# One queue in strict turn instead of two queues side by side, in a one-pass gradient of a 268 MB array

## The chip, the cores and the metric

The kernel runs on one core of a Trainium2 chip; the other cores are idle. The metric is device time in microseconds (us).

Some words for what follows. HBM is the large memory that holds input and output, SBUF the core's own memory. Data go between them by 16 DMA engines, which all take part in each transfer. A *packet* is what the profile records as one move of one engine, here mostly 64 KB. A transfer has *landed* when the last of the 16 engines is done with it; the *spread* is the time from the first engine to the last. The *turn* is the place where a queue goes from a load to the store behind it.

## The reference

```python
x = np.random.randn(8192, 8192).astype(np.float32)     # 268 MB
def reference(x):
    return np.gradient(x, axis=1)   # inside: (x[j+1] - x[j-1]) / 2; at both ends: a one-sided difference
```

Each input byte has to be loaded once and each output byte stored once: 536.9 MB in all.

## The kernel before

256 rows are one *set* of 8.39 MB: two rows per partition, 64 KB in each of 128 partitions. There are 32 sets and three slots in SBUF. GpSimd (POOL) puts the four edge differences of each pair of rows aside, VectorE (DVE) makes the halved central difference of the whole set in one pass and in place, and a small copy puts the edges back. Then the set is stored from the same slot.

```python
R, NB, SH = 2, 3, 64            # rows per partition, slots, shift of the input within a slot
# ... slots, semaphores ld[k], st[k] (one per slot), counters ...

def load(i):
    k = i % NB
    if i < NB:
        parts = [(ld[k], 0, R)]
    else:
        nc.sync.wait_ge(ld[(i - 1) % NB], 16 * ld_n[(i - 1) % NB])   # the load before has landed
        nc.sync.wait_ge(st[k], 16 * st_n[k])                         # store i-3 has landed
        parts = [(ld[k], 0, R)] if i < nsets - 1 else [(ld_rows[r], r, 1) for r in range(R)]
    for sem, r0, nr in parts:
        nc.sync.dma_start(out=slots[k][...], in_=x_sets[i, ...]).then_inc(sem, 16)
    ld_n[k] += 1

# work(i, ..., placer, storer, sem): DVE pass, edge copy on `placer`, store issued by `storer`

for i in range(NB):
    load(i)
for i in range(nsets):
    k = i % NB
    if i < nsets - 1:
        ready = put_aside(i, 0, R, ld[k], 16 * ld_n[k])
        placer = nc.scalar if i % 2 else nc.vector
        storer = nc.scalar if i + NB < nsets else nc.sync
        work(i, 0, R, ready, placer, storer, st[k])
        st_n[k] += 1
    else:                                  # the last set goes in two half loads and two half stores
        for r in range(R):
            ready = put_aside(i, r, 1, ld_rows[r], 16)
            work(i, r, 1, ready, nc.vector, nc.sync, st_rows[r])
    if i + NB < nsets:
        load(i + NB)
```

Loads are issued by SyncE (SP), and the stores of sets 0 to 28 by ScalarE (ACT), each on its own queue. The stores of the last three sets are on SP, behind the last load. I write L5 and S5 for the load and the store of set 5.

## Time and profile before

| | before |
|---|---|
| time, median of 3 runs | 1252.09 us (1250.42 to 1253.31) |
| traffic | 536.9 MB, 429 GB/s over the span |
| VectorE busy | 44% of the span |

The head of the page of the kernel before: span, VectorE's busy share, the DMA engines' busy tenths in 40 slices, what they moved in each slice, the packets and the queues (q1 is SP's, q10 is ACT's).

```profile
span 1252.1 us, 254 instructions
...
DVE 554.2 (44%) x51; ACT 4.2 (0%) x16; POOL 15.1 (1%) x37
...
DMA  9999999999999999999999999999999999999998
GB/s 402 435 435 433 433 433 435 435 431 427 435 421 433 431 435 431 435 435 429 433 435 435 435 435 429 431 429 427 429 421 435 431 431 435 433 433 435 376 437 371
DMA packets 9506, 536.88 MB, mean 429 GB/s; under 512 B 1057, under 2 KB 1057, under 8 KB 1057
...
q1 hardware_dynamic: 5328, 293.60, 54.7%
q10 hardware_dynamic: 4176, 243.27, 44.8%
```

The DMA engines are busy in every slice; the last three slices have two low ones (376 and 371 GB/s). The 1056 smallest packets are the semaphore increments: 66 transfers times 16 engines (one more is not the kernel's). The Trainium skill, "DMA: Bandwidth & Descriptors", section "Why a DMA increments its semaphore by 16 and not by 1", says that each of the 16 engines posts its own increment after its own data, and that only the full 16 tells that all has landed. The trace agrees.

Three pieces of the chain of waits of the kernel before (start, length, what): loads land 36 to 42 us apart in the steady part, 38.70 us on average from 209 to 1138 us.

```profile
1062.92 38.63 DMA slot<-in_x_dram
1101.57 36.20 DMA slot<-in_x_dram
1137.78 31.38 DMA slot<-in_x_dram
```

Stretches near the end of the kernel before, the windows view (stretch, length, busy time of three engines with counts, clock, DMA share, GB/s):

```profile
core 0: us, DVE busy (x) ACT busy (x) POOL busy (x), PEclk, DMA share, GB/s
1160.00:1165.00 5.00, 0.00 (x0) 0.00 (x0) 0.00 (x0) 1.00 0.97 419
1165.00:1170.00 5.00, 0.54 (x1) 0.00 (x0) 0.20 (x1) 1.00 0.15 66
1170.00:1175.00 5.00, 5.00 (x1) 0.00 (x0) 0.00 (x0) 1.00 1.09 419
1240.00:1245.00 5.00, 0.00 (x0) 0.00 (x0) 0.00 (x0) 1.00 0.99 426
1245.00:1250.00 5.00, 0.00 (x0) 0.00 (x0) 0.00 (x0) 1.00 0.74 321
```

From 1165 to 1170 us the DMA engines are nearly empty, by this view for 5 x (1 - 66/419) = 4.2 us. S28 and L30 have run out, L31 waits, and S29, though computed, stands behind L31 on SP.

The timeline of the kernel before around this place (start, length, engine, line, operation):

```profile
1169.23 0.20 POOL L84 TENSOR_TENSOR ends<-slot 128x4 f32<-128x4 f32 x1 [31.19 <-DMA slot<-in_x_dram]
...
1170.03 34.81 SPq L118 DMA_DIRECT2D out_dram<-slot  x4
1181.27 5.47 POOL L84 TENSOR_TENSOR ends<-slot 128x2 f32<-128x2 f32 x1 [11.84 <-DMA slot<-in_x_dram]
...
1192.28 3.25 POOL L84 TENSOR_TENSOR ends<-slot 128x2 f32<-128x2 f32 x1 [5.54 <-DMA slot<-in_x_dram]
```

The first line is the landing of L30, the second SP's first store after it has issued L31 at last. The third and fourth are the landings of L31's two halves, 11.0 us apart, where 4.19 MB should take half of a set's 19.3 us.

### The profile page before, as it was taken

Reading aid. Unit: us, or ns where it says so; the run is one execution under the profiler, and the core shown is the slowest. Engines: PE = TensorE matmul, PEld = TensorE weight load, DVE = VectorE, ACT = ScalarE, POOL = GpSimd, SP = SyncE. Lnnn points to the kernel's source line nnn. Section 1 sums busy time; section 2 is a strip of 40 time slices with the busy share of each in tenths; the row PEclk is TensorE's granted clock in tenths of the full one; section 3 lists DMA queues with packets and bytes.
Section 4 is the critical chain, followed back from the end, with each engine's and each line's share of the span. In section 5 each row is a group of like instructions: output and inputs, shape, how many; then the busy total and the mean of one; then the engine's idle time right before and its main releaser. Section 6 shows DMA issues by size and latency. Waiting matters only on the chain.

```text
span 1252.1 us, 254 instructions
## 1 busy us (share of the span) xinstructions
DVE 554.2 (44%) x51; ACT 4.2 (0%) x16; POOL 15.1 (1%) x37
## 2 busy tenths in 40 slices
DVE  2841553345542455333554235543355523555640
ACT  0000000000000000000000000000000000000000
POOL 0000000000000000000000000000000000000110
DMA  9999999999999999999999999999999999999998
GB/s 402 435 435 433 433 433 435 435 431 427 435 421 433 431 435 431 435 435 429 433 435 435 435 435 429 431 429 427 429 421 435 431 431 435 433 433 435 376 437 371
DMA packets 9506, 536.88 MB, mean 429 GB/s; under 512 B 1057, under 2 KB 1057, under 8 KB 1057
## 3 DMA queue, kind: packets, MB, share of 16 engines
q1 hardware_dynamic: 5328, 293.60, 54.7%
q10 hardware_dynamic: 4176, 243.27, 44.8%
q14 instruction: 2, 0.01, 0.0%
HBM read 268.44 MB, written 268.44 MB: 429 GB/s over the span
## 4 chain that ended last, share of the span: by engine, by line
DMA 92%; DVE 4%; issue 0%; POOL 0%; SPq 0%
DMA slot<-in_x_dram 89%; DVE slot L102 4%; DMA out_dram<-slot 3%; DVE slot L116 0%; POOL ends L84 0%; SPq L168 0%; SPq L69 0%; SPq L42 0%
## 5 line engine op out<-in xcount | busy, mean ns | idle before, releaser
L102 DVE CUSTOM_DVE_ANT_0 slot<-slot 128x16382 f32<-128x16382 f32 (+1 forms) x33 | 551.3, 16706 | 649.7 <-POOL ends L84 649.7
L84 POOL TENSOR_TENSOR ends<-slot 128x4 f32<-128x4 f32 (+1 forms) x33 | 14.9, 452 | 1180.2 <-DMA slot<-in_x_dram 1180.2
L116 ACT COPY slot<-ends 128x4 f32<-128x4 f32 x15 | 3.0, 198 | 1110.0 <-DVE slot L102 1110.0
L116 DVE COPY slot<-ends 128x4 f32<-128x4 f32 (+1 forms) x18 | 3.1, 171 | 0.6
L116 ACT ACT_TABLE_LOAD x1 | 1.3, 1283 | 41.3 <-DVE slot L116 41.3
L157 POOL MEMSET const-bfloat16-1.0<- 128x1 bf16 x1 | 0.1, 102 | 0.0
L157 POOL MEMSET const-uint8-127<- 128x1 uint8 x1 | 0.1, 102 | 0.0
L157 POOL MEMSET const-float32-0.0<- 128x1 f32 x1 | 0.1, 99 | 0.2 <-issue 0.2
L157 POOL MEMSET const-float32-1.0<- 128x1 f32 x1 | 0.1, 99 | 0.0
## 6 DMA issues: line engine op xcount, KB each, us to landing
slot<-in_x_dram SPq DMA_DIRECT2D x2, 4096.0 KB, 17.3
out_dram<-slot SPq DMA_DIRECT2D x2, 4096.0 KB, 45.3
slot<-in_x_dram SPq DMA_DIRECT2D x31, 38.6
out_dram<-slot ACTq DMA_DIRECT2D x29, 40.2
out_dram<-slot SPq DMA_DIRECT2D x2, 42.8
```

The lines of the kernel that those rows point to most:

```text
L84: nc.gpsimd.tensor_sub(out=ends[:, i, r0 : r0 + nr, :], in0=xin[:, :, 1 : m : m - 2], in1=xin[:, :, 0 : m - 1 : m - 2],),
L102: nc.vector._custom_dve(dve_ops.TENSOR_TENSOR_REDUCE_SUB_MAX, out=mid, in0=after, in1=before, s0=0.0, s1=0.5,),
L116: at = done(copy(out=to, in_=of), placed[placer])
L157: nc = _bacc.Bacc("TRN2", target_bir_lowering=False, num_devices=1)
```

## The change

Its intent is to have loads and stores take strict turns on one queue, with fewer instructions and without waits that the queue's order makes needless.

```diff
             else:
-
-                nc.sync.wait_ge(ld[(i - 1) % NB], 16 * ld_n[(i - 1) % NB])
                 nc.sync.wait_ge(st[k], 16 * st_n[k])
@@
             if i < nsets - 1:
                 ready = put_aside(i, 0, R, ld[k], 16 * ld_n[k])
-                placer = nc.scalar if i % 2 else nc.vector
-                storer = nc.scalar if i + NB < nsets else nc.sync
-                work(i, 0, R, ready, placer, storer, st[k])
+                work(i, 0, R, ready, nc.scalar, nc.sync, st[k])
                 st_n[k] += 1
@@
-            if i + NB < nsets:
-                load(i + NB)
+
+            if i > 0 and i - 1 + NB < nsets:
+                load(i - 1 + NB)
```

The queue's order is now L0 L1 L2 S0 S1 L3 S2 L4 S3 L5 and so on; at the end S29, L31 in two halves, S30, S31 in two halves.

## The prediction

> **What bounds the kernel now.** The DMA engines. The page's slice table shows DMA at 9 in 39 of 40 slices; the whole is 536.9 MB at 429 GB/s. VectorE is busy 44%. In the chain of waits, load landings follow each other every 38.70 us from 209 to 1138 us (24 sets of 16.78 MB, 433.6 GB/s). The Trainium skill, "DMA: Bandwidth & Descriptors", section "Where 436 GB/s comes from", gives a ceiling of 435.2 GB/s; the trace agrees (two loads alone land 19.32 us apart in the timeline, 434 GB/s). 536.9 MB at 435.2 GB/s is 1233.6 us, so 18.5 us is all there is to win.
>
> **Where those 18.5 us are.** Start: the first load lands at 23.1 us, 3.8 more than its 19.3. End: in the last 82.1 us (from the issue at 1170.0) 33.55 MB move, 77.1 us at the ceiling: 5.0 us of latency and completion. Just before, 1165 to 1170 moves 66 GB/s (windows view), about 4.2 us empty: store 28 and load 30 had run out, and everything else stood behind load 31, which waits for store 28. Some 6 us are spread: short dips (229 GB/s in 62 to 64 us), 0.15 us per set.
>
> **What changes.** All stores move from ACT's queue to SP's; the wait of a load for the load before goes; load i+2, not i+3, is issued after store i. The queue's order is S1 L3 S2 L4 S3 L5... Edge copies of all sets but the last go to ACT (0.198 us, not 0.171), off the path.
> - Does the queue run dry? With 19.3 us per transfer, store 3 is issued some 19 us after load 3 landed (POOL 0.20, DVE 17.22, copy 0.2, hops), with load 4 (and store 2) ahead. Load 5 is issued when store 2 lands, again with load 4 ahead: 17 us or more of work stays queued. At the start loads 1 and 2 cover computation 0; at the end store 30 covers the last 8.68 us. The 4.2 us gap disappears.
> - Do turns lower the rate? Before, the engines should alternate between two busy queues packet by packet (same page, "Queues, rings and completion order"; packets are mostly 64 KB), so each already switched direction many times per set and lost 0.15 us. Loads alone ran at 434 GB/s, and the last 82 us already are one SP queue, two half loads and four stores, at the ceiling. Some 60 changes of direction should cost almost nothing.
>
> **Sum (estimate from trace durations).** 64 transfers of 19.32 us are 1236.5, plus 3.8 start, plus about 1 after the last landing: 1241.3. I predict **1242 us**, range **1237 to 1250**. Faster by over 2% needs 1227 us, less than the traffic at the ceiling: chance 0.01. Within 2%: 0.95. Slower: 0.04.
>
> **What would show each step.** Right: ACT's queue gone; landings of loads 38.6 us apart; no slice at 376 near the end; 433 to 435 GB/s nearly everywhere; SP waits for stores and edge copies while DMA never empties. Wrong on starvation: SP waiting for the edge copy while the DMA share falls. Wrong on turns: 39 us or more between landings with DMA at 9, or a dip at each change of direction.
>
> **What would make it wrong.** A fixed drain at each change of direction: 0.3 us each cancels the gain, 0.7 us makes it over 1% slower. Engines drifting apart, so that the slowest decides each landing (the last half loads land 11.0 us apart, not 9.6). A bounded ring holding up SP. Pure writes to HBM slower than mixed traffic; the tail's 58 us of stores say no.

## More of the kernel before

The time of a run is 1.7 to 2.2 us longer than its span, from its first to its last instruction (for instance 1253.98 us of time for a profiled span of 1252.1 us).

## The result, and the profile after

| | before | after |
|---|---|---|
| time, median of the runs beside each other | 1252.70 us (1250.42 to 1256.05, 4 runs) | 1252.36 us (1251.24 to 1252.88, 4 runs) |
| ratio, 95% interval | | 0.9994 (0.9970 to 1.0018) |
| span of the profiled run | 1252.1 us | 1249.5 us |

A ratio is the mean time of one kernel's fast runs over that of the other's of the same rounds, so it is not quite the ratio of the medians. A later set of five rounds gave 0.9991 (0.9977 to 1.0005). The change is worth nothing that these runs can tell; the intervals leave room for 0.3%.

The head of the page of the changed kernel:

```profile
span 1249.5 us, 225 instructions
...
DMA  9999999999999999999999999999999999999997
GB/s 403 436 436 418 428 430 436 434 430 436 432 436 434 436 434 432 432 432 420 434 436 432 434 436 432 436 434 436 436 430 436 436 434 422 428 436 436 436 434 330
DMA packets 9505, 536.88 MB, mean 430 GB/s; under 512 B 1056, under 2 KB 1056, under 8 KB 1056
...
q1 hardware_dynamic: 9504, 536.88, 99.5%
```

ACT's queue is gone. The slice of 376 GB/s near the end is gone too; 436 and 434 stand where the kernel before had 376 and 437. But the last slice fell from 371 to 330. Some pieces of the chain of waits of the changed kernel; each starts at the landing of a load:

```profile
120.79 0.07 issue
...
159.90 0.07 issue
...
472.33 0.07 issue
...
899.83 0.07 issue
...
938.50 0.07 issue
```

The first two are neighbours, 39.11 us apart; from 120.79 to 472.33 us there are nine sets, 39.06 us each, more than the 38.6 that I had predicted. The last two are neighbours again, 38.67 us apart. Something costs 0.4 us per set in the first third of the run and nothing in the last. The same five stretches as before, in the changed kernel:

```profile
1160.00:1165.00 5.00, 0.00 (x0) 0.00 (x0) 0.00 (x0) 1.00 0.97 419
1165.00:1170.00 5.00, 0.00 (x0) 0.00 (x0) 0.00 (x0) 1.00 1.00 433
1170.00:1175.00 5.00, 4.38 (x1) 0.00 (x0) 0.20 (x1) 1.00 0.97 419
1240.00:1245.00 5.00, 0.00 (x0) 0.00 (x0) 0.00 (x0) 1.00 0.38 164
1245.00:1250.00 5.00, 0.00 (x0) 0.00 (x0) 0.00 (x0) 1.00 0.07 28
```

The empty place at 1165 us is gone, as predicted. But from 1240 to 1250 us the engines move little for almost ten microseconds. That is not a gap, as there is nothing left to issue: some engines have finished and some have not.

The 16 landing times of each transfer, taken from the trace, show it plainly. This is the time between the first and the last of the 16 engines to finish a load in the changed kernel, and the total by which the packets near that load's end are longer than the usual 2.418 us, summed over the engines, for ten of the loads:

```
load landed at us       62.5  120.8  159.9  198.8  277.4  433.2  628.0  822.5 1015.8 1131.6
first to last engine     0.4    0.5    0.9    1.2    2.5    3.5    5.2    6.4    6.5    6.5
excess, sum of engines  16.4    4.6    1.2    1.4    4.5    1.7    0.6    2.6    0.0    0.1
```

The excess packets are not anywhere in the run: apart from small ones in the first 260 us, all groups of packets longer than 2.45 us are the last packets of a load, just where the queue turns from a load to the store behind it. At the first such turn all 16 engines lose about 1 us. Later turns hit the engines unequally. The engines come apart, and once they are 6.5 us apart, nearly no packet is long any more (the largest later sum is 1.1 us, at 938 us).

What that does to the end, from the 16 landings of the very last transfer:

| last transfer | mean of the 16 engines | last engine | last minus mean |
|---|---|---|---|
| before | 1249.9 us | 1250.3 us | 0.4 us |
| after | 1243.3 us | 1247.7 us | 4.4 us |

The average engine did gain 6.6 us: 3.2 of idle time in the gap, 3.3 of stretched packets (6.9 us per engine after the first 20 us before, 3.6 after), and 0.1 of small items. The kernel is over when the last engine is, and that one gained 2.6.

### The profile page after: what moved, and what is told of

Same layout as the page of the kernel before. It is cut to its first block, busy times and chain, and to the rows that moved or that the text cites. A ratio compares the mean times of both kernels' runs of the same rounds, so it can differ in the third digit from the quotient of the medians.

```text
span 1249.5 us, 225 instructions
## 1 busy us (share of the span) xinstructions
DVE 551.7 (44%) x35; ACT 7.4 (1%) x32; POOL 6.8 (1%) x37
## 4 chain that ended last, share of the span: by engine, by line
another core or an unknown queue 78%; DMA 15%; DVE 3%; POOL 0%; issue 0%; ACT 0%; SPq 0%
DMA slot<-in_x_dram 9%; DMA out_dram<-slot 7%; DVE slot L100 3%; POOL ends L82 0%; ACT slot L114 0%; DVE slot L114 0%; SPq L165 0%; SPq L42 0%
## 5 line engine op out<-in xcount | busy, mean ns | idle before, releaser
L114 ACT COPY slot<-ends 128x4 f32<-128x4 f32 x31 | 6.1, 198 | 1179.8 <-DVE slot L100 1179.8
L82 POOL TENSOR_TENSOR ends<-slot 128x4 f32<-128x4 f32 (+1 forms) x33 | 6.6, 199 | 1202.2 <-DMA slot<-in_x_dram 1202.2
```

The source lines that it names most:

```text
L82: nc.gpsimd.tensor_sub(out=ends[:, i, r0 : r0 + nr, :], in0=xin[:, :, 1 : m : m - 2], in1=xin[:, :, 0 : m - 1 : m - 2],),
L114: at = done(copy(out=to, in_=of), placed[placer])
```

## The experiments

The theories, as they stood before the runs. **T (turns):** the last packets of a load are stretched where the queue turns from load to store, as long as the engines are in step; the loss is unequal, so that the engines come apart and the slowest decides the end. **D (drift):** some engines are simply slower, whatever the direction. **W (warm-up):** the stretching belongs to the first 800 us of a run. Fourteen kernels were run; "right" means that the output agreed with the reference.

### All transfers loads

```diff
             storer.wait_ge(*at)
+            if i < nsets - 1:      # wrong output on purpose: a load of the same set instead of its store
+                storer.dma_start(out=b[:, r0 * m : (r0 + nr) * m],
+                                 in_=x_sets[i, :, r0 * m : (r0 + nr) * m]).then_inc(sem, 16)
+                return
             storer.dma_start(out=out_sets[...], in_=b[...]).then_inc(sem, 16)
```

> The changed kernel with the stores of all sets but the last turned into loads of the same 8 MB into the same slot (wrong output on purpose): same queue, same dependencies, same bytes, one change of direction in the whole run. Theory T (in the changed kernel the last load packet of an engine is stretched by up to 1.2 us when the queue turns from a load to a store, the less the further the 16 engines are apart, and this costs the slowest engine 6.5 us): the 16 engines stay within 1 us of each other, nearly no 64 KB packet after the first 20 us is longer than 2.45 us, landings 19.34 us apart, span about 1243 (one turn at the end, up to 1 us). Rival D (some engines are simply slower, whatever the direction): the spread of the 16 landings grows to about 6.5 us again and the span is about 1249.5.

### All transfers stores

```diff
             for sem, r0, nr in parts:
+                if i >= NB:        # wrong output on purpose: a store of the slot instead of a load
+                    nc.sync.dma_start(out=out_sets[i, :, r0 * m : (r0 + nr) * m],
+                                      in_=slots[k][:, SH + r0 * m : SH + (r0 + nr) * m]).then_inc(sem, 16)
+                    continue
                 nc.sync.dma_start(out=slots[k][...], in_=x_sets[i, ...]).then_inc(sem, 16)
```

> The changed kernel with all loads but the first three turned into stores of the same slot (wrong output on purpose): one turn, after the third load. Theory T: one stretch of about 1 us per engine at that turn, then none; spread of the landings below 1.5 us to the end; landings 19.34 us apart; span about 1243. Rival D: spread grows to about 6.5 us, span about 1249.5. Rival S (stores to HBM are slower than loads): landings over 19.5 us apart with all engines together.

Measured, one each: 1246.10 us with loads alone and 1246.14 us with stores alone. Their outputs are wrong, which doesn't matter for the times. From the pages, the one with loads first:

```profile
span 1244.3 us, 225 instructions
...
GB/s 404 438 438 430 413 438 438 438 438 438 438 413 430 438 438 438 438 438 419 423 438 438 438 438 438 426 417 438 438 438 438 438 430 413 438 438 438 438 438 371
...
HBM read 528.48 MB, written 8.39 MB: 431 GB/s over the span
```

```profile
span 1244.4 us, 225 instructions
...
GB/s 404 434 430 419 436 438 438 438 438 436 432 423 428 438 438 438 438 438 434 430 419 436 438 438 438 438 434 421 426 438 438 438 438 423 419 438 438 438 438 371
...
HBM read 25.17 MB, written 511.71 MB: 431 GB/s over the span
```

The 16 engines stay 0.3 to 0.5 us apart from 60 us to the end with loads, and 0.6 to 0.9 us with stores; landings are 19.3 us apart in both. With stores, the one turn at 58 us stretched all 16 last load packets, by 16.5 us in sum, and nothing after it was over 0.05 us long. The end of the all-loads run in the windows view:

```profile
1240.00:1245.00 5.00, 0.00 (x0) 0.00 (x0) 0.00 (x0) 1.00 0.25 107
1245.00:1250.00 5.00, 0.00 (x0) 0.00 (x0) 0.00 (x0) 1.00 0.00 0
```

It falls off within 1240 to 1245, where the changed kernel took until 1247.7 us. D is out: with the same bytes, queue and dependencies the engines don't come apart when the queue doesn't turn. (The repeat of the changed kernel ran on another chip; but the kernel with two queues below ran on the same chip as these two, and there the engines came apart.) Loads alone and stores alone are equally fast, so my fear of slow pure writes is out too.

### Kept in step at every turn

```diff
                 nc.sync.wait_ge(st[k], 16 * st_n[k])
+                nc.sync.wait_ge(st[(i - 2) % NB], 16 * st_n[(i - 2) % NB])
```

> The changed kernel, and each load also waits for the newest store, so that the 16 engines run dry and start together before every load-store pair. Theory T: since the engines are in step at every turn, all 16 last load packets are stretched at every turn, about 0.6 to 1.2 us each, to the end of the run, not only in the first 800 us; with some 2 us of emptiness and a slow first packet per pair, landings of loads are 41.5 to 43 us apart instead of 38.7, span 1330 to 1370. Rival W (the stretches belong to the first 800 us of a run and die out by themselves): no stretched packets after 850 us, landings then about 1 us closer together than at the start.

Measured: 1357.97 us, one look, right. Three landings of loads late in the run, from its timeline:

```profile
1060.83 0.20 POOL L83 TENSOR_TENSOR ends<-slot 128x4 f32<-128x4 f32 x1 [42.33 <-DMA slot<-in_x_dram]
...
1103.99 0.20 POOL L83 TENSOR_TENSOR ends<-slot 128x4 f32<-128x4 f32 x1 [42.96 <-DMA slot<-in_x_dram]
...
1146.36 0.20 POOL L83 TENSOR_TENSOR ends<-slot 128x4 f32<-128x4 f32 x1 [42.17 <-DMA slot<-in_x_dram]
```

They are 43.2 and 42.4 us apart, where the changed kernel has 38.7. The engines are 0.4 to 1.0 us apart throughout, and at every turn, to the end, all 16 last load packets are stretched: 16 to 24 us in sum, 1.0 to 1.5 us per engine. As T expected. But it is not quite the same turn as in the changed kernel, since here the queue has run dry before each load; later turns of the changed kernel cost 0.6 to 4.6 us in sum. So W was not out yet; the last two runs below settle that.

### The new order, with the stores on ACT's queue

```diff
-                work(i, 0, R, ready, nc.scalar, nc.sync, st[k])
+                work(i, 0, R, ready, nc.scalar, nc.scalar if i + NB < nsets else nc.sync, st[k])
```

> The changed kernel with its stores, but for the last three sets', issued on ACT's queue again: the new order and the dropped wait of the loads without the one queue. Loads may now run beside stores and ahead of them. Theory T: stretches are now where either direction begins beside the other and not at the end of loads; total cost on the slowest engine of the same kind; time within 0.4% of before (1247 to 1257). If strict turns on one queue mattered by themselves, this would differ from the changed kernel by more than that.

Measured: 1252.47 us (1248.52 to 1257.26, 4 runs), ratio 0.9978 (0.9956 to 1.0001), right. No difference that can be told from the changed kernel, so within some 0.3% the single queue by itself isn't what matters. The profiled run was its slowest (1257.26 us); there the engines were 12.7 us apart at the end, last minus mean 9.9 us, more than in the changed kernel. Two queues do not cure the lag, and here they made it uneven from run to run.

### The changed kernel again

> The changed kernel as it is, to have it beside the next three on one chip. Expected: within 0.4% of before, spread of the 16 landings at the end 6 to 7 us.

Measured: 1251.89 us (1251.03 to 1252.72, 5 runs), ratio 0.9991 (0.9977 to 1.0005). Engines 7.4 us apart at the end (6.5 in the first profile), last minus mean 4.4 us, the same as in the first profile.

### Half as many turns

```diff
-            if i > 0 and i - 1 + NB < nsets:
-                load(i - 1 + NB)
+            if i % 2:
+                for j in (i - 1 + NB, i + NB):
+                    if j < nsets:
+                        load(j)
```

> The changed kernel with the queue's order L L S S L L S S, so half as many turns from load to store (16 instead of 31). Theory T: stretches only at the end of every second load; if each turn adds to the slowest engine what is left until the engines are 6.5 us apart, half as many turns leave the engines 4 to 6.5 us apart at the end and save 0 to 2.5 us (1249 to 1252.5). If the queue ran dry in this order, the span would be over 1255.

Measured: 1251.33 us (1249.87 to 1252.10, 5 runs), ratio 0.9984 (0.9970 to 0.9999), right. Against the 1251.89 of the changed kernel on the same chip it saved half a microsecond, within the noise. Stretches were only at the ends of every second load, as expected, but the engines still ended 6.9 us apart, slightly more than I had expected. The spread grew more slowly (3.6 us at 588 us, where the repeat of the changed kernel had 5.6) and had longer to grow, as stretching went on to the last turn (3.7 us in sum at 1201 to 1206 us). So 16 turns and 31 cost about the same here.

### Half as long packets

```diff
-                parts = [(ld[k], 0, R)]
+                parts = [(ld[k], r, 1) for r in range(R)]        # likewise for the later loads
@@
-            storer.dma_start(out=out_sets[i, :, r0 * m : (r0 + nr) * m], in_=...).then_inc(sem, 16)
+            for r in range(r0, r0 + nr):
+                storer.dma_start(out=out_sets[i, :, r * m : (r + 1) * m], in_=...).then_inc(sem, 16)
```

> The changed kernel with each 8 MB transfer issued as two transfers of one row each, in the same order L L S S per set: same turns, same bytes, packets of 32 KB (1.21 us) instead of 64 KB (2.42 us). Theory T with the spread that ends the stretching counted in packets (6.5 us is 2.7 packets): spread at the end about 3.3 us, time 3 us less than the changed kernel (about 1249). If the spread is a time, not a number of packets: 6.5 us again and no gain.

Measured: 1253.82 us (1252.77 to 1256.13, 5 runs), ratio 1.0014 (0.9997 to 1.0030), right. The spread at the end was 6.3 us, so it is not counted in packets, and my hope of a gain fell. Packets of 32 KB took 1.213 us, which is 0.3% more per byte than 2.418 us for 64 KB; that alone would be some 4 us over 512 packets of 64 KB per engine (an estimate: 512 x 2 x 1.213 = 1242.1 instead of 1238.0). The loss seen is half of that, 1.9 us between the medians. Late in the run, where little is stretched, a set took 38.73 us here and 38.67 us in the repeat of the changed kernel, which over 32 sets is 1.9 us.

### The kernel before, without its gap

```diff
-                storer = nc.scalar if i + NB < nsets else nc.sync
+                storer = nc.scalar
```

> The kernel before with the stores of the last three sets left on ACT's queue, so that they don't stand behind the last load: the gap of 4.2 us at 1165 us should be gone, and nothing else of the change is in. My prediction counted the gap as 4.2 us of time. Theory T: the average engine stood idle there, but the slowest engine for only about 1.3 us (its last packet ends at 1168.8, the next begins at 1170.1), and closing the gap leaves the engines apart to the end: the time falls by 0 to 2 us, not by 4, and the spread at the end is 3 to 9 us instead of 0.6.

Measured: 1248.90 us (1247.39 to 1251.65, 6 runs), ratio 0.9970 (0.9956 to 0.9985), right. This is a miss of my second thoughts: the gap was worth 0.3%, 1.9 to 5.5 us of 1253.5, more than the 0 to 2 expected, and in line with the 4.2 us of the first prediction. The stretch that held the gap, in its windows view:

```profile
1165.00:1170.00 5.00, 0.00 (x0) 0.00 (x0) 0.00 (x0) 1.00 1.03 446
```

It moved 446 GB/s where the kernel before moved 66. The profile fell on its slowest run (1251.65 us), so its ends say little of the faster ones; in it the last half store had to wait for the last half load, which landed only at 1227.6 us beside S30, and the landings of the last transfer were 0.2 us apart, not the 3 to 9 expected (they had been 6.5 us apart at the half load before).

### A copy inside SBUF instead of the store, and a copy inside HBM

```diff
-            storer.dma_start(out=out_sets[i, :, r0 * m : (r0 + nr) * m], in_=b[:, r0 * m : (r0 + nr) * m])
+            inside = i < nsets - 1                       # wrong output on purpose
+            # either: out=b[:, m : 2 * m],  in_=b[:, 0:m]            (SBUF to SBUF, 4 MB)
+            # or:     out=out_sets[i, ...], in_=x_sets[i, ...]       (HBM to HBM, 8 MB)
```

> The changed kernel with the stores of all sets but the last replaced by a copy of one row of the slot onto the other, inside SBUF (4 MB, wrong output on purpose). At the turn that cost 16 us summed over the engines in the changed kernel, the transfers now go from HBM-to-SBUF to SBUF-to-SBUF: only what is read from changes, nothing is written to HBM. Theory Read (the last load packets are stretched because the packets behind them read from SBUF, not from HBM): all 16 last packets of a load before a copy stretched by about 1 us at the first turn. Theory Write (they are stretched because the packets behind them write to HBM): no stretch at the ends of loads.

> The changed kernel with the stores of all sets but the last replaced by copies from the input to the output inside HBM (8 MB, wrong output on purpose). At the turn the transfers go from HBM-to-SBUF to HBM-to-HBM: only what is written to changes. Theory Read: no stretch at the ends of loads. Theory Write: stretched by about 1 us per engine at the first turn. The copies themselves may be slower than stores; the span is not what is looked at.

Measured: 947.69 us with copies inside SBUF (406.9 MB), 1409.73 us with copies inside HBM. Their outputs are wrong, which doesn't matter for the times. Neither theory came through whole. With SBUF copies, all the last load packets were stretched at the first turn (15.0 us in sum), and at none of the later ones, with the engines 0.5 us apart to the end. With HBM copies the last load packets were not stretched at all; the copies were slow from their first packet to their last (a load and a copy landed 44 us apart, so 24.5 us for a copy of 8.39 MB instead of 19.3). The engines came apart all the same, from 0.5 us at the third load to 8.4 us at the end; so they can part without stretched ends of loads, and stretching is the way seen in the changed kernel, not the only one. At the first turn it is enough that the packets behind the load read from SBUF. For the later turns neither reading from SBUF alone nor writing to HBM alone brings the stretching about. What it is that delays the last packets stays open.

### The dropped wait alone

```diff
-                nc.sync.wait_ge(ld[(i - 1) % NB], 16 * ld_n[(i - 1) % NB])     # in the kernel before
```

> The kernel before without the wait of a load for the load before it: one part of the change alone. My sum gave that part no time of its own: within 0.3% of before (1249 to 1257), the gap before the last load still there.

Measured: 1259.08 us (1256.75 to 1262.39, 4 runs), ratio 1.0041 (1.0023 to 1.0059), right. That is 0.4% slower, a little beyond what I had expected. Its windows view near the end:

```profile
1165.00:1170.00 5.00, 0.00 (x0) 0.00 (x0) 0.00 (x0) 1.00 0.09 39
1170.00:1175.00 5.00, 0.00 (x0) 0.00 (x0) 0.00 (x0) 1.00 0.06 26
1175.00:1180.00 5.00, 0.00 (x0) 0.00 (x0) 0.00 (x0) 1.00 0.84 315
```

The thin stretch before L31 has become more than twice as long, and it is lag again: 39 and 26 GB/s is the work of one or two engines (433.7 / 16 = 27 GB/s each). The first engine finished S28 at 1154.8 us and the last at 1175.1; L31 now waits for S28's last engine, and all that is left stands behind L31. So the wait by itself was no cost that could simply be dropped. The changed kernel can drop it because with its queue and its order nothing that is ready stands behind a load that isn't.

### One store more on ACT

```diff
-                storer = nc.scalar if i + NB < nsets else nc.sync      # in the kernel before
+                storer = nc.scalar if i + NB <= nsets else nc.sync
```

> The kernel before with the store of set 29 left on ACT's queue and the last two sets' stores on SP: closes the gap that the last load makes, without the end of the run with every store on ACT, in which the last half load had to share the engines with store 30. Expected: no dip near 1165 us; the engines no longer set equal by the gap, so 3 to 6 us of lag of the slowest engine behind the mean at the end; time 0 to 5 us less than before (about 1249 beside 1253), so about the same as with all three stores on ACT.

Measured: 1250.97 us (1249.39 to 1256.47, 6 runs), ratio 0.9972 (0.9958 to 0.9985), right. As expected: the gap is closed by moving S29 alone, the gain is the same 0.3%, and in the profiled run (again the slowest) the last engine was 3.7 us behind the mean at the end, where the kernel before has 0.4.

### In step once, late, and once, early

```diff
                 nc.sync.wait_ge(st[k], 16 * st_n[k])
+                if i == 24:        # in the other run: 12
+                    nc.sync.wait_ge(st[(i - 2) % NB], 16 * st_n[(i - 2) % NB])
```

> The changed kernel, and only the load of set 24, at about 930 us, when stretching has died out, also waits for the newest store, so that the engines run dry and start together once. Theory T: stretched packets at the ends of loads come back in the turns after it (1 to 5 us summed over the engines each, after a first turn of about 18) and the spread grows again from 0.6 us to 2 to 5 us at the end. Rival W: after the restart's own first turn no packets are stretched, and the spread stays below 1.5 us to the end. Time 3 to 9 us above the changed kernel in T, 3 to 5 in W.

> The same with the load of set 12, at about 470 us. Theory T: the spread, some 4 us by then, falls to 0.6 us and grows again as it did from the start of the changed kernel, over some 700 us, to 5 to 6.5 us at the end; stretching lasts past 820 us. Rival W: the spread grows as fast as it would have without the restart, that is by 2 to 2.5 us more until 820 us, then stops.

Measured, one look each, right: 1256.55 and 1258.38 us, beside 1256.31 us for one run of the kernel before. The time from the first to the last engine, by the landing of the load:

```
restart at set 24:  landed at us   433.8  665.8  897.6  940.2  979.1 1057.0 1096.3 1135.6 1174.9  end
                    first to last    3.8    3.9    3.9    0.8    0.7    1.3    1.8    2.4    2.8  3.5
restart at set 12:  landed at us   433.8  476.4  515.3  554.6  594.4  672.9  789.5  906.3 1061.5  end
                    first to last    3.9    0.6    0.8    1.3    2.3    3.3    3.9    4.7    5.3  5.3
```

After the restart the stretched packets come back. In the run with the late one only five packets were long from 630 us to the restart, 0.6 us in sum. After it the restart's own turn had 20.6 us and the six that followed 2.1 to 4.3 us each:

```
late restart, long packets at the ends of loads (us, how many engines, excess in sum):
 776.2  1  0.07 |  815-816  3  0.44 |  893  1  0.11 | restart | 936  16  20.57 |
 975-976 16 4.31 | 1014-1015 12 2.49 | 1053-1054 13 2.08 | 1092-1093 13 3.83 | 1130-1132 12 3.55 | 1169-1172 11 2.51
```

W is out: the stretching does not end by the time since the start. That it ends because the engines are apart fits all of this but isn't shown by itself, as the restart also empties the queue. The spread at which it ends is not fixed: 6.5 us and 7.4 us in two profiles of the changed kernel, 4.0 us here.

## Why the prediction was right or wrong

**Bound by the DMA engines, nothing to win beyond 18.5 us: right.** The ceiling was a little lower than the one I used. The Trainium skill, "DMA: Bandwidth & Descriptors", section "Where 436 GB/s comes from", gives 435.2 GB/s for the 16 ports; a 64 KB packet took 2.418 us in nearly all cases, and 16 x 65,536 B / 2.418 us is 433.7 GB/s, so 1238.0 us and not 1233.6 for the traffic.

**The queue never runs dry: right.** In the changed kernel, with each packet matched to the end of the one before it, no engine waits more than 0.35 us between its first packet and its last.

**The gap disappears: right,** if for the other of the two waits, and with 3.2 us for the average engine rather than 4.2. Closing it alone, in the kernel before, gave 0.3%.

**"Some 60 changes of direction should cost almost nothing": wrong, and this is the step that failed.** The long packets at the ends of loads cost the average engine 3.4 us in all, 1.0 of it at the first turn, and the slowest engine then ends 4.4 us behind the average. The cost is real: in the repeat of the changed kernel the long packets sum to 1.1 us more per engine, and the average engine ends 1.1 us later. Beside the all-loads run the average engine ends only 1.0 us later (1243.3 against 1242.3) and the slowest 5.1 us (1247.7 against 1242.5), but that run is no clean zero: its packets take 2.422 us at the median, and its transfers land 19.35 us apart instead of 19.32. I had two reasons. The first, that the engines of the kernel before switch all the time at no cost, was not looked at closely: its packets are stretched too, and more, by the 6.9 us per engine given above. (It was not all wrong. With the packets matched end to start, an engine there changes queue some 130 to 190 times from 300 to 1100 us, an estimate, and its long packets in that time sum to 3.7 us. So a change of queue at one packet costs little on average.) The second was that its last 82 us "already are one SP queue, two half loads and four stores, at the ceiling". That stretch has one turn in it, and the turn shows, in a line that I had read and quoted: the landings of the half loads 11.0 us apart. The trace gives the reason. All 16 last packets of the second half load took 2.05 to 2.34 us where 1.213 is usual, about 1 us per engine. I had booked that microsecond as latency. In the changed kernel, where the engines are apart at this place, the same halves land 9.69 us apart:

```profile
1199.37 0.20 POOL L82 TENSOR_TENSOR ends<-slot 128x2 f32<-128x2 f32 x1 [28.78 <-DMA slot<-in_x_dram]
...
1209.06 0.20 POOL L82 TENSOR_TENSOR ends<-slot 128x2 f32<-128x2 f32 x1 [9.49 <-DMA slot<-in_x_dram]
```

**"Engines drifting apart, so that the slowest decides each landing"** stood in the prediction among what would make it wrong, and that is what happened. Each engine has its own share of the bytes (with the packets of the all-loads run matched end to start, 33.55 MB for each of the 16), and the skill (same page, section "Two DMAs through the same engine are not ordered") says "Nothing at all orders DMAs across the 16 engines." The trace agrees: in one queue and with the same work they came 6.5 us apart. In the kernel before, the gap at 1165 us had set them equal again (0.6 us apart at the end), so the gap had covered part of the same loss. Removing it uncovered that. How much it covered is not shown: there the spread had been 9.4 us at 848 us and had shrunk to 2.6 us at the landing of L30, just before the gap, for a reason that no run tells.

**The size of the miss** (predicted 1241.3 before rounding, 1251.2 in the profiled run):

| term | predicted | measured | difference |
|---|---|---|---|
| landing of the first load | 23.1 us | 22.85 us | -0.3 |
| pace of a transfer without long packets, 63 more times | 19.32 us | 19.32 us (five sets from 938.50 to 1131.65 us, 38.63 us for the two transfers of each) | 0.0 |
| long packets, average engine | 0 | 3.6 us after the first 20 us, 3.4 of it at the turns | +3.6 |
| slowest engine behind the average | 0 | 4.4 us, against 0.3 at the first load | +4.1 |
| last landing to the end of the span | 1.0 us | 1.8 us | +0.8 |
| time outside the span | 0 | 1.7 us | +1.7 |

The sum is +9.9. The turns and the lag that they leave are over 7 us of it. As a check, 22.5 us (the mean landing of the first load) + 63 x 19.32 + 3.6 is 1243.3 us, the mean landing measured. The last line is a slip of reading: the span of the kernel before's profile (1252.1) looks like its median time (1252.09) only because the profiled run was a slow one of 1253.98.

**Where the expected gain went,** profile to profile: the average engine gained 6.6 us, by the gap and by less stretching; the lag of the last engine behind the average took back 4.0; 2.6 us of span remain, and the timed runs show about 0.1%, with an interval that includes zero. Closing the gap alone did better: on the chip where both ran, the kernel before without its gap took 1248.90 us and the changed kernel 1251.89. So the rest of the change (one queue, the new order, the dropped wait) seems to cost about what the gap gives, though the intervals of the two ratios (0.9956 to 0.9985 and 0.9977 to 1.0005) still overlap.

**What stays open.** Why the last packets of a load are delayed; which of the 16 engines lose most, since the trace doesn't name the engine of a packet; at what spread the stretching ends (with two queues the engines were up to 21 us apart in mid-run), and why the engines also part beside copies inside HBM. No version with the right output beats the 1246 us of the runs without turns. The two that close the gap in the kernel before (ratios 0.9970 and 0.9972) beat the kernel before, and by their medians both kernels, though the second ran on another chip than the repeat of the changed kernel.

## What to carry to other kernels

When DMA is busy all the time, ask for the slowest of the 16 engines and not for the average: a gap that is removed may have been the place where the engines waited for each other, and the gain then shows in the average and not in the end. Take a stretch of the old trace as evidence that something is free only after each of its landings has been accounted for; a landing 1.3 us late was the very cost in dispute. And test a disputed cost by taking it out altogether, as with transfers all in one direction: that gave 1246 us.

## What the Trainium skill lacked or had wrong

- No page has a cost of turning one queue from loads to stores ("DMA: Bandwidth & Descriptors" would be the place). Measured: about 1.0 us for each of the 16 engines at a turn with the engines in step after three loads (16.4 us in sum), 1.0 to 1.5 us where the queue had run dry before the load, 0.04 to 0.3 us (0.6 to 4.6 in sum) at later turns, and 0 to 1.1 us in sum with the engines 6.5 us apart.
- The same page says that the engines are not ordered among themselves, but not how far they come apart on one queue with equal work: 6.5 and 7.4 us after 1250 us here, 8.4 us with copies inside HBM in place of the stores, 0.4 us with loads alone, 0.6 us with stores alone.
- The same page, section "Where 436 GB/s comes from", has 435.2 GB/s; packets of 64 KB took 2.418 us at the median in the changed kernel and with stores alone, which is 433.7 GB/s for 16 engines, and 2.422 us with loads alone, 432.9 GB/s.
- The same page has no rate for copies inside HBM with rows laid out as here, 64 KB each and end to end: 8.39 MB took about 24.5 us, 342 GB/s of bytes copied, where a load takes 19.3 us.
